# A decoder layer on one core: where the down weights' sums are formed, the order of the first gates, and what a later pool's tiles wait for

## The chip, the core and the metric

The kernel runs on one core of a Trainium2 chip. The metric is the time of one execution on the device, in microseconds: the median of three runs is 1895.49 us (1895.41 to 1898.42). The engines are TensorE (PE in the rows; PEld is its loading of weights), VectorE (DVE), ScalarE (ACT), GpSimd (POOL) and SyncE (SP), which only issues DMAs. Each engine works through its instructions in order; an instruction that waits holds all that stand behind it on that engine, the DMAs that the engine issues included.

## The reference, cut to what matters

One layer of a decoder, 1024 positions by 1024 channels, in float32. The first sub-layer normalises x, runs four causal mixers (A: sparse attention, B: dilated windows, C: forgetting attention, D: latent attention), and then gates, sums and projects their outputs. The second is a gated feed-forward network with a causal convolution of width 3.

```python
h = rms_norm(x, g1)
o = [A(h), B(h), C(h), D(h)]                       # 256, 128, 256, 256 channels
merged = sum(sigmoid(h @ w_gate[i]) * (o[i] @ w_branch[i]) for i in range(4))
x = x + rms_norm(merged @ w_out, g2)
f = rms_norm(x, g3)
up, gate = split(f @ w_up)                         # 2816 channels each
y = activation(causal_conv3(gate)) * up
x = x + rms_norm(y @ w_down, g4)
```

## The kernel before, in words

Every product is kept near float32: each operand is split into a high part (a cast to fp32r on ACT, `split_weights`) and a low part (raw minus high, on DVE or POOL), and three matmuls stand for one (`gemm`). Activations are held with channels on the partitions; a matmul has 128 channels in, 128 out and 512 positions.

**Stage 1, the attention** (pool `attn`), has a prologue in which h is formed, the projections run and the keys and queries are prepared, and then the softmax blocks of the four mixers. Where TensorE would stand, it takes matmuls of the fillers: `fill_tile` computes one tile of branch 1's gates (48 matmuls `pf`), with its weights loaded by SP, cast by ACT (`fh`), and their low part `fl` formed by POOL; the tanh goes to `gate_d` in memory. There are eight; they have low priority, and what is left of them is done at the end of the stage.

**The sums for the last product.** The feed-forward network's down projection is done in a form with fewer products, which needs sums and differences of quarters of its weights. `down_sums` (L218 to L231) forms them ahead on POOL, in the prologue of stage 1: for each of 11 blocks two loads of 128x1024 (`draw`, L224), four operations of 128x512 (L226 to L229) and two stores into `wt_d` (L231). The tiles have the tags `whi` and `wlo` of the pool of weights, two buffers each.

**Stage 2, the gates** (pool `p2`). It begins with branch 1, whose gates are loaded back from `gate_d` (`te`, L1118, into tiles of the tag "c", four buffers); `add_branch` multiplies with the branch's weights and adds into `merged` by one DVE operation (STT, L1008). `load_output` (L984 to L991) brings a mixer's output: a load into `oraw` (one buffer, issued by ACT), a cast `oh` (ACT) and `ol` (DVE). Two tiles of branch 3 have plain gates (`plain`, L1111 and L1122 to L1130). `make_sums` (L1045 to L1072) forms sums of quarters of h on DVE. Then come pairs j = 1 to 11, each two gate tiles by seven products in place of eight: X[j] (gx, two products), gy (S2, S3), gz (S1, A22), gw (S4), then the branch product gp. `gate_sets(j+1)` (L1023 to L1036) is prepared meanwhile: sums of the raw gate weights on POOL (s1 L1028, L1029, L1030, L1035), casts on ACT (L960), low parts on POOL or DVE (L961), in six slots. Pairs 4 and 8 begin a new branch and load its output first.

**Stages 3 and 4** (pools `p3`, `p4`) are the output projection with norm and residual, and the feed-forward network; the last product reads `wt_d`.

What is written in the program is then put in order for each engine by a scheduler with priorities. A tile of a pool that opens later waits until the earlier pool whose memory it takes is done as a whole.

Of the kernel before, what the change touches and what calls it, by code (L numbers as in the profile page):

```python
# [15 lines left out]
F32 = mybir.dt.float32  # L16
# [3 lines left out]
ALU = mybir.AluOpType  # L20
# [3 lines left out]
D = 1024  # L24
# [62 lines left out]
def body(tc, a, out):  # L87
# [31 lines left out]
    def split_weights(hi, lo, raw, eng, scale):  # L119
        if scale == 1.0:  # L120
            A.copy(hi, raw)  # L121
            eng.tensor_tensor(lo, raw, hi.bitcast(F32), op=ALU.subtract)  # L122
        else:
            A.mul(hi, raw, scale)
            eng.tensor_scalar(raw, raw, scale, None, op0=ALU.mult)
            eng.tensor_tensor(lo, raw, hi.bitcast(F32), op=ALU.subtract)

    def load_weights(src, shape, pool_=None, scale=1.0, eng=None):

        pool_ = pool_ or wp  # L130
# [43 lines left out]
    def h_half(hf):  # L174
        return lambda kt: (H[hf][0][:, kt], H[hf][1][:, kt])


    with ExitStack() as c1:
# [36 lines left out]
            if i is not None:  # L215
                fill_tile(i)

        def down_sums(jj):  # L218


            w = [wp.tile([128, D], F32, name="draw", tag=("whi", "wlo")[jj % 2], bufs=2) for _ in range(2)]
            for c in range(2):
                f = 128 * (NH * c + jj)
                G.dma_start(w[c], a["wdn"][f:f + 128, :])  # L224
            l, r = slice(0, 512), slice(512, 1024)
            G.tensor_tensor(w[1][:, r], w[1][:, r], w[0][:, r], op=ALU.subtract)  # L226
            G.tensor_tensor(w[0][:, r], w[0][:, r], w[0][:, l], op=ALU.subtract)
            G.tensor_tensor(w[0][:, l], w[0][:, l], w[1][:, r], op=ALU.add)
            G.tensor_tensor(w[1][:, l], w[0][:, l], w[1][:, l], op=ALU.subtract)  # L229
            for c in range(2):  # L230
                G.dma_start(wt_d[jj][c], w[c])  # L231


        def weights_tm(src):

# [77 lines left out]
            SP.dma_start(t, bass.AP(tensor=src.tensor, offset=src.offset + 127, ap=[[1280, 128], [1, 1152]]))  # L313
            return t

        def project(src, scale=1.0, eng=G):

            hi, lo = load_weights(src, [KT, 128], scale=scale, eng=eng)
            for hf in range(2):
                ps = bank()  # L320
                gemm(ps, lambda kt: (hi[:, kt, :], lo[:, kt, :]), h_half(hf), range(KT))
                yield hf, ps
# [193 lines left out]
        KCL = ap.tile([128, 64], F32R, name="KCL")  # L516
        VC = ap.tile([128, 128], F32R, name="VC")
        kvc = ap.tile([128, S], F32, name="kvc", tag="vt", bufs=BUFS["vt"])
        for hf, ps in project(a["win"][0], eng=V):
            A.copy(kvc[:, cs(hf)], ps)  # L520
        blk = [tile4("blk", "vs", (128, 16, 2, 64), F32) for _ in range(2)]
        posT = ap.tile([128, 32], F32, name="posT")
# [9 lines left out]
        for e in range(2):  # L532
            G.memset(blk[e], 0.0)
            for d in range(2):
                r = slice(64 * d, 64 * d + 64)
                V.tensor_tensor(blk[e][r, :, d, 0:63], kv3[r, :, e:e + 63],
                                posT[r, 16 * e:16 * e + 16].unsqueeze(2).to_broadcast([64, 16, 63]), op=ALU.add)
        for jj in range(NH):
            down_sums(jj)
        fill()  # L540

        for i in range(4):
            V.tensor_copy(sm[:, 2 * i:2 * i + 2], tm[i][:, :, 128:176])
        qn = [(tile4("qnhi", "qs"), tile4("qnlo", "qs")) for _ in range(2)]
        lss = ap.tile([128, 2, 8], F32, name="lss")
        kinds = ((0, 128, [kvn], 2), (176, 256, qn, 0))
# [6 lines left out]
        for i, (c0, n, dst, gc) in enumerate(kinds):  # L553
            for b in range(8):
                t = tm[b // 2][:, b % 2, c0:c0 + n]
                V.tensor_scalar(t, t, lss[:, i, b:b + 1], None, op0=ALU.mult)
        for i, (c0, n, dst, gc) in enumerate(kinds):
            for k in range(n // 128):
                for hb in range(2):
# [8 lines left out]

        rotate(sm[:, :, None, 0:32], (0, 8, 1), ap.tile([128, 4, 128], F32, name="rt", tag="th", bufs=BUFS["th"]))

        krt = wp.tile([128, 8, 96], F32, name="krt", tag="wraw", bufs=2)
        V.memset(krt[:, :, 0:64], 0.0)
        V.tensor_copy(krt[:, :, 64:96], sm[:, :, 0:32])
        krt2 = tile4("kr", "vt")
        kr = [krt2[64:96], krt2[96:128]]
# [6 lines left out]
        wkv = tile4("wkv", "P", (128, 2, 512))  # L582
        raw = wp.tile([128, 512], F32, name="wraw", tag="wraw", bufs=2)
        SP.dma_start(raw, a["wukv"])
        split_weights(wkv[:, 0], wkv[:, 1], raw, V, 1.0)
        wq = [tile4("wq", "P", (128, 2, 384)) for _ in range(2)]
        raw = wp.tile([128, 2, 384], F32, name="wraw", tag="wraw", bufs=2)
        SP.dma_start(raw, a["wuq"])
        split_weights(wq[0], wq[1], raw, V, 1.0)

        gate = ap.tile([128, 8, 12], F32, name="gate")
        A.activation(gate, sm[:, :, 32:44], AF.Tanh, scale=0.5)
# [320 lines left out]
        A.dma_start(o_d[256:384, :], ot0)  # L913


    hq = ctx.enter_context(pool("hq"))
    merged = [hq.tile([128, KT, 512], F32, name=f"mg{hf}", tag="g", bufs=2) for hf in range(2)]
    psq = ctx.enter_context(pool("psq", space=PSUM))

    def pq(name, tag="q"):  # L920
        return psq.tile([128, D], F32, name=name, tag=tag, bufs=2)
# [44 lines left out]
        gemm(ps, lambda k: (t[:, 0, 128 * k:128 * k + 128], t[:, 1, 128 * k:128 * k + 128]),  # L966
             lambda k: (bh[:, k], bl[:, k]), range(4))

    with pool("p2") as p2:
        branches = ((1, 256, 1), (3, 640, 2), (0, 0, 2), (2, 384, 2))  # L970
        kt0 = {br: f0 // 128 for br, f0, _ in branches}
        O, pairs = {}, [(br, p) for br in (3, 0, 2) for p in range(4)]
# [28 lines left out]
        def add_branch(br, m, hf, t, pb, bw, nk):  # L1001


            c = slice(512 * hf, 512 * hf + 512)
            gemm(pb, lambda k: (bw[0][:, m % 2, k], bw[1][:, m % 2, k]),
                 lambda k: (O[br, k][0][:, c], O[br, k][1][:, c]), range(nk))
            if br == 1:
                V.scalar_tensor_tensor(merged[hf][:, m], t, 1.0, pb, op0=ALU.add, op1=ALU.mult)  # L1008
            else:
                V.scalar_tensor_tensor(t, t, 1.0, pb, op0=ALU.add, op1=ALU.mult)  # L1010
                V.tensor_tensor(merged[hf][:, m], merged[hf][:, m], t, op=ALU.add)

        def raw_gates(j):
            if j not in raws and j < len(pairs):
# [93 lines left out]

        lo_f, hi_f = slice(0, 512), slice(512, 1024)
        load_output(*branches[0])  # L1110
        plain = [load_weights(a["wg"][3, m], [KT, 128]) for m in range(2)]  # L1111
        for p in range(4):
            bw = branch_weights(1, p, 1)
            for m in (2 * p, 2 * p + 1):
# [4 lines left out]
                    add_branch(1, m, hf, t, ps[:, (lo_f, hi_f)[hf]], bw, 1)  # L1119
        load_output(*branches[1])  # L1120
        bw = branch_weights(3, 0, 2)
        for m, (gh, gl) in enumerate(plain):  # L1122
            for hf in range(2):
                ps = pq("pgb", "qr"[hf])
                gemm(ps[:, lo_f], lambda k: (gh[:, k], gl[:, k]), h_half(hf), range(KT))
                t = c_tile("tg")
                A.activation(t, ps[:, lo_f], AF.Tanh, scale=0.5)
                add_branch(3, m, hf, t, ps[:, hi_f], bw, 2)
# [18 lines left out]
        for _ in range(2):
            load_wo()

# [3 lines left out]

    hs = ctx.enter_context(pool("hs"))

    def operand(t):
        return t[:, 0:4], t[:, 4:8]

    B = {"11": None, "21": operand(hs.tile([128, KT, 512], F32R, name="b21"))}
    with pool("p3") as p3:

        def put(jobs):

# [149 lines left out]
        put([job("2", 3), job("3", 3)])  # L1315
        put([job("1", 3), job("4", 3)])

    with pool("p4") as p4:
        slot_p4 = lambda: p4.tile([128, 2, 512], F32R, name="aset", tag="as", bufs=8)
        cw = p4.tile([128, 2 * NJ, 4], F32, name="cw")  # L1320
        SP.dma_start(cw, a["convw"])
# [298 lines left out]
```

## Time and profile before

| | |
|---|---|
| median of three runs | 1895.49 us (1895.41 to 1898.42) |
| profiled execution | 1898.08 us, span 1896.3 us |
| granted clock of TensorE, mean | 0.972 |
| PE busy | 1794.0 us (95%) |
| DVE, ACT, POOL busy | 1275.2, 850.5, 648.6 us |
| DMA | 180.09 MB, mean 95 GB/s |

The span is the time from the first to the last instruction; the run is 1.8 us longer. Busy times overlap. PE is the engine with the most work by far, so a microsecond counts where PE stands or runs at a lower granted clock. The granted clock has two levels, 1.2 and 2.4 GHz; 0.74 for a stretch means that about half of it was at the lower one. In the rows, "idle before <- releaser" is time in which an engine had nothing to do until the named instruction was done.

### The profile page before, as it was taken

Reading aid. Unit: us, or ns where it says so; the run is one execution under the profiler, and the core shown is the slowest. Engines: PE = TensorE matmul, PEld = TensorE weight load, DVE = VectorE, ACT = ScalarE, POOL = GpSimd, SP = SyncE. Lnnn points to the kernel's source line nnn. Section 1 sums busy time; section 2 is a strip of 40 time slices with the busy share of each in tenths; the row PEclk is TensorE's granted clock in tenths of the full one; section 3 lists DMA queues with packets and bytes.
Section 4 is the critical chain, followed back from the end, with each engine's and each line's share of the span. In section 5 each row is a group of like instructions: output and inputs, shape, how many; then the busy total and the mean of one; then the engine's idle time right before and its main releaser. Section 6 shows DMA issues by size and latency. Waiting matters only on the chain. (4 is left out here: it accounts for less than half of the span.)

```text
span 1896.3 us, 24478 instructions
## 1 busy us (share of the span) xinstructions
PE 1794.0 (95%) x8644; PEld 1453.3 (77%) x8644; DVE 1275.2 (67%) x2413; ACT 850.5 (45%) x1622; POOL 648.6 (34%) x638
## 2 busy tenths in 40 slices
PE   8885999999999999788999999989999999999997
PEld 7754777777777778566888888778888888888886
DVE  5535886999888626384555565669767676677757
ACT  5323555665666545133333343444434344454444
POOL 1347522121111230106444410248676767400110
PEclk9877999999999999999999999989999999999999
DMA  7178311010001111332211123232222222194235
GB/s 261 60 227 269 141 46 47 25 58 13 24 22 47 61 45 35 108 125 63 74 60 53 59 93 141 78 102 78 80 87 78 90 78 84 57 332 125 88 105 183
DMA packets 70634, 180.09 MB, mean 95 GB/s; under 512 B 11040, under 2 KB 16496, under 8 KB 70512
## 3 DMA queue, kind: packets, MB, share of 16 engines
q1 hardware_dynamic: 50992, 121.73, 19.9%
q10 hardware_dynamic: 13184, 33.73, 4.9%
q0 software_dynamic: 6336, 23.07, 3.5%
q8 instruction: 68, 1.11, 0.2%
q14 instruction: 54, 0.44, 0.1%
HBM read 139.09 MB, written 43.67 MB: 96 GB/s over the span
## 5 line engine op out<-in xcount | busy, mean ns | idle before, releaser
L411 ACT ACTIVATE P<-P,nm 128x512 f32<-128x512 f32 (+7 forms) x160 | 107.9, 676 | 65.6 <-DVE nm L406 64.8
L449 ACT CAST th<-ptp 128x512 fp32r<-128x512 f32 (+3 forms) x202 | 97.1, 518 | 83.8 <-PE ptp L443 72.3
L1251 POOL TENSOR_TENSOR aset<-sums,aset 128x512 fp32r<-128x512 f32 x66 | 129.7, 1965 | 7.3 <-ACT aset L1250 6.8
L144 PE MATMUL pd<-hh,whi 128*128 128x512 f32 x320 | 129.3, 404 | 2.0 <-DVE kl L344 2.0
L450 DVE TENSOR_TENSOR tl<-ptp,th 128x512 fp32r<-128x512 f32 (+3 forms) x202 | 115.5, 600 | 21.0 <-ACT th L449 18.9
L146 PE MATMUL pd<-hh,wlo 128*128 128x512 f32 x320 | 129.2, 404 | 0.0
L145 PE MATMUL pd<-hl,whi 128*128 128x512 f32 x320 | 127.8, 399 | 0.0
L443 PE MATMUL ptp<-miscc,P 128*128 128x128 f32 x678 | 114.1, 277 | 10.7 <-DVE P L420 4.8
L1474 PE MATMUL pk<-aset 128*128 128x512 f32 x308 | 120.3, 394 | 1.2 <-DVE part L1554 0.8
L1475 PE MATMUL pk<-aset 128*128 128x512 f32 x308 | 120.3, 390 | 1.3 <-DVE aset L122 1.1
L1476 PE MATMUL pk<-aset 128*128 128x512 f32 x308 | 119.5, 390 | 0.0
L447 POOL MEMSET th<- 128x128 f32 x86 | 19.2, 224 | 272.9 <-PE pvt L458 121.8
L1250 ACT CAST aset<-wraw 128x512 fp32r<-128x512 f32 x88 | 54.0, 617 | 101.1 <-PE pz L146 37.4
L443 PEld LDWEIGHTS ptp<-miscc,P 128*128 128x128 f32 x678 | 81.1, 142 | 23.5 <-DVE P L420 6.6
L1250 ACT CAST aset<-sums 128x512 fp32r<-128x512 f32 x66 | 40.7, 620 | 120.3 <-PE py L146 32.8
L121 ACT CAST aset<-r 128x512 fp32r<-128x512 f32 x77 | 47.7, 620 | 97.6 <-PE pk L1476 87.6
L122 DVE TENSOR_TENSOR aset<-r,aset 128x512 fp32r<-128x512 f32 x77 | 55.5, 721 | 51.4 <-ACT aset L121 51.4
L960 ACT CAST aset<-wraw 128x512 fp32r<-128x512 f32 x66 | 40.7, 621 | 99.4 <-PE gx L146 41.2
L1266 POOL TENSOR_TENSOR sums<-wraw 128x512 f32<-128x512 f32 x22 | 30.8, 1402 | 127.9 <-PE pk L146 101.4
L961 POOL TENSOR_TENSOR aset<-wraw,aset 128x512 fp32r<-128x512 f32 x33 | 43.7, 1325 | 89.5 <-ACT aset L960 89.5
L458 PE MATMUL pvt<-th,vs 128*128 128x256 f32 x238 | 69.2, 303 | 2.8 <-DVE ot L468 2.5
L1474 PEld LDWEIGHTS pk<-aset 128*128 128x128 f32 x308 | 57.8, 188 | 17.3 <-DVE part L1554 1.5
(451 smaller groups left out, 5679.2 us busy)
## 6 DMA issues: line engine op xcount, KB each, us to landing
wraw<-in_wup SPq DMA_DIRECT2D x44, 512.0 KB, 3.6
wraw<-in_wg SPq DMA_DIRECT2D x24, 512.0 KB, 3.5
draw<-in_wdn POOLq DMA_DIRECT2D x22, 512.0 KB, 4.4
wt_d<-draw POOLq DMA_DIRECT2D x22, 512.0 KB, 3.8
act_d<-o ACTq DMA_DIRECT2D x22, 512.0 KB, 3.7
r<-act_d SPq DMA_DIRECT2D x44, 256.0 KB, 5.4
wraw<-wt_d SPq DMA_DIRECT2D x44, 256.0 KB, 2.6
wraw<-in_win SPq DMA_DIRECT2D x20, 512.0 KB, 3.3
```

The costliest lines, as they stand in the source:

```text
L144: T.matmul(ps, lh, rh, start=first and ii == 0, stop=False)
L145: T.matmul(ps, lh, rl, start=False, stop=False)
L146: T.matmul(ps, ll, rh, start=False, stop=last and ii == n - 1)
L411: A.activation(P[:, 0:c0], P[:, 0:c0], AF.Exp, bias=prev, scale=-1.0, accum_out=den)
L443: T.transpose(tp[0:kr, at[x]], P2[x[1]][:, c:c + kr], ident)
L449: A.copy(th[0:kr, i0:i1], tp[0:kr, i0:i1])
L450: V.tensor_tensor(tl[0:kr, i0:i1], tp[0:kr, i0:i1], th[0:kr, i0:i1].bitcast(F32), op=ALU.subtract)
L1250: A.copy(t[:, 0], src)
L1251: eng.tensor_tensor(t[:, 1], src, t[:, 0].bitcast(F32), op=ALU.subtract)
L1474: T.matmul(ps[b], at[:, 0, c], wt[:, 0], start=st, stop=False, skip_group_check=not first)
L1475: T.matmul(ps[b], at[:, 0, c], wt[:, 1], start=False, stop=False, skip_group_check=not first)
L1476: T.matmul(ps[b], at[:, 1, c], wt[:, 0], start=False, stop=sp, skip_group_check=not first)
```

## The change

Four things are changed; the arithmetic stays the same.

1. `down_sums` leaves the prologue. It is called in stage 2 after each pair, for two halves at a time, 22 in all. A half works in one tile of 128x4x256 of the tag `oraw`, which has one buffer and is also that of `load_output`: two loads, four operations of 128x256, two stores, all issued by POOL. Rows in memory are 1 KB long instead of 4 KB, and there are 88 DMAs of 256 KB instead of 44 of 512 KB.
2. In the prologue some copies, half of the scalings of `tm`, a memset and the low parts of three weights go from DVE to POOL; `krt` takes the tag `whi`.
3. The plain gates of branch 3, m = 0, are computed ahead of branch 1's additions; their results stay in PSUM and in two of the four "c" tiles until branch 3. `make_sums` is called ahead of branch 1, and the weights of m = 1 are loaded after it.
4. The pools `hq`, `psq`, `p2`, `hs`, `p3` and `p4` are opened with `reuse_waits="tile"`: a tile waits only for the tiles whose memory it takes.

```diff
-        def down_sums(jj):
-            w = [wp.tile([128, D], F32, name="draw", tag=("whi", "wlo")[jj % 2], bufs=2) for _ in range(2)]
...
-        for jj in range(NH):
-            down_sums(jj)
         fill()
         for i in range(4):
-            V.tensor_copy(sm[:, 2 * i:2 * i + 2], tm[i][:, :, 128:176])
+            G.tensor_copy(sm[:, 2 * i:2 * i + 2], tm[i][:, :, 128:176])
...
                 t = tm[b // 2][:, b % 2, c0:c0 + n]
-                V.tensor_scalar(t, t, lss[:, i, b:b + 1], None, op0=ALU.mult)
+                (G if b % 2 else V).tensor_scalar(t, t, lss[:, i, b:b + 1], None, op0=ALU.mult)
...
-        krt = wp.tile([128, 8, 96], F32, name="krt", tag="wraw", bufs=2)
-        V.memset(krt[:, :, 0:64], 0.0)
+        krt = wp.tile([128, 8, 96], F32, name="krt", tag="whi", bufs=2)
+        G.memset(krt[:, :, 0:64], 0.0)
...
-        split_weights(wkv[:, 0], wkv[:, 1], raw, V, 1.0)
+        split_weights(wkv[:, 0], wkv[:, 1], raw, G, 1.0)
...
-        split_weights(wq[0], wq[1], raw, V, 1.0)
+        split_weights(wq[0], wq[1], raw, G, 1.0)
...
-    hq = ctx.enter_context(pool("hq"))
+    hq = ctx.enter_context(pool("hq", reuse_waits="tile"))
...
+        sums_of = iter((jj, u) for jj in range(NH) for u in range(2))
+        def down_sums(n):
+            for jj, u in [next(sums_of) for _ in range(n)]:
+                w = p2.tile([128, 4, 256], F32, name="draw", tag="oraw", bufs=1)
+                cols = lambda x: x.rearrange("p (h u t) -> p h u t", h=2, u=2)[:, :, u]
+                for c in range(2):
+                    f = 128 * (NH * c + jj)
+                    G.dma_start(w[:, 2 * c:2 * c + 2], cols(a["wdn"][f:f + 128, :]))
+                G.tensor_tensor(w[:, 3], w[:, 3], w[:, 1], op=ALU.subtract)
+                G.tensor_tensor(w[:, 1], w[:, 1], w[:, 0], op=ALU.subtract)
+                G.tensor_tensor(w[:, 0], w[:, 0], w[:, 3], op=ALU.add)
+                G.tensor_tensor(w[:, 2], w[:, 0], w[:, 2], op=ALU.subtract)
+                for c in range(2):
+                    G.dma_start(cols(wt_d[jj][c]), w[:, 2 * c:2 * c + 2])
...
-        plain = [load_weights(a["wg"][3, m], [KT, 128]) for m in range(2)]
+        def plain_gates(m):
+            gh, gl = load_weights(a["wg"][3, m], [KT, 128])
+            t = []
+            for hf in range(2):
+                ps = pq("pgb", "qr"[hf])
+                gemm(ps[:, lo_f], lambda k: (gh[:, k], gl[:, k]), h_half(hf), range(KT))
+                t.append((ps, c_tile("tg")))
+                A.activation(t[hf][1], ps[:, lo_f], AF.Tanh, scale=0.5)
+            return t
+        first = plain_gates(0)
+        T1, T2, T3, t4 = make_sums()
         for p in range(4):
             bw = branch_weights(1, p, 1)
...
-        for m, (gh, gl) in enumerate(plain):
...
-            if m == 0:
-                T1, T2, T3, t4 = make_sums()
+        for hf, (ps, t) in enumerate(first):
+            add_branch(3, 0, hf, t, ps[:, hi_f], bw, 2)
+        gh, gl = load_weights(a["wg"][3, 1], [KT, 128])
...
             combine(j)
+            down_sums(2)
```

The other pools of point 4 change in the same way, and `project` loses its argument `eng` (the first projection's weights are split on POOL, too).

How this moves instructions on POOL in the gate stage: before, one pair's worth of rows between two s1 (`aset` are low parts of the sets, `wraw` the raw gates):

```order
L1028 TENSOR_TENSOR s1_9270<-wraw_9105 128x512
L1029 TENSOR_TENSOR wraw_9105<-wraw_9103,wraw_9105 128x512
L961 TENSOR_TENSOR aset_9100<-wraw_8928,aset_9100 128x512
L1030 TENSOR_TENSOR wraw_9103<-s1_9270,wraw_9103 128x512
L1035 TENSOR_TENSOR wraw_9103<-wraw_9103 128x512
L961 TENSOR_TENSOR aset_9274<-wraw_9103,aset_9274 128x512
L961 TENSOR_TENSOR aset_9277<-wraw_9105,aset_9277 128x512
L961 TENSOR_TENSOR aset_9280<-s1_9270,aset_9280 128x512
```

Now, while the set of pair 6 is prepared (`draw` is a half, `wt_d` its store):

```order
L1031 TENSOR_TENSOR wraw_9234<-s1_9407,wraw_9234 128x512
L1012 DMA wt_d4_95<-draw_9551 256x1x256
L1036 TENSOR_TENSOR wraw_9234<-wraw_9234 128x512
L1006 DMA draw_9560<-in_wdn 128x2x256 x2
L944 TENSOR_TENSOR aset_9411<-wraw_9234,aset_9411 128x512
L1007 TENSOR_TENSOR draw_9560<-draw_9560 128x256
L944 TENSOR_TENSOR aset_9414<-wraw_9236,aset_9414 128x512
L1008 TENSOR_TENSOR draw_9560<-draw_9560 128x256
L1009 TENSOR_TENSOR draw_9560<-draw_9560 128x256
L1010 TENSOR_TENSOR draw_9560<-draw_9560 128x256
L1012 DMA wt_d4_95<-draw_9560 256x1x256 x2
L944 TENSOR_TENSOR aset_9417<-s1_9407,aset_9417 128x512
```

Of the operations of a set, some now stand between a half's loads and its stores, and s1 of the next set stands behind whole halves.

And on DVE at the start of stage 2: before, STTs of branch 1 (`mg`) and operations of `make_sums` (`t`) take turns from the beginning:

```order
L1047 TENSOR_TENSOR t_8562<-hh1_128,hl1_129 128x2048
L1047 TENSOR_TENSOR t_8563<-hh0_126,hl0_127 128x2048
L122 TENSOR_TENSOR ol_8326<-oraw_8323,oh_8325 128x1024
L122 TENSOR_TENSOR bw_8343<-bw_8341,bw_8342 128x256
L1048 TENSOR_TENSOR t_8563<-t_8562,t_8563 128x2048
L1008 SCALAR_TENSOR_TENSOR mg0_8315<-te_8349,pgb_8348 128x512
L1008 SCALAR_TENSOR_TENSOR mg0_8315<-te_8362,pgb_8361 128x512
L1047 TENSOR_TENSOR t_8564<-hh1_128,hl1_129 128x2048
L1008 SCALAR_TENSOR_TENSOR mg1_8316<-te_8355,pgb_8348 128x512
L1008 SCALAR_TENSOR_TENSOR mg1_8316<-te_8368,pgb_8361 128x512
```

Now the operations of `make_sums` come in a block:

```order
L1049 TENSOR_TENSOR t_8287<-t_8281,t_8279 128x1024
L1048 TENSOR_TENSOR t_8288<-hh0_126,hl0_127 128x1024
L1049 TENSOR_TENSOR t_8281<-t_8281,t_8280 128x2048
L1049 TENSOR_TENSOR t_8294<-t_8280,t_8293 128x2048
L1049 TENSOR_TENSOR t_8288<-t_8288,t_8281 128x1024
L1048 TENSOR_TENSOR t_8289<-hh0_126,hl0_127 128x1024
L1049 TENSOR_TENSOR t_8302<-t_8281,t_8301 128x2048
L1049 TENSOR_TENSOR t_8289<-t_8289,t_8281 128x1024
L122 TENSOR_TENSOR bw_8313<-bw_8311,bw_8312 128x256
L1049 TENSOR_TENSOR t_8306<-t_8286,t_8305 128x1024
L1049 TENSOR_TENSOR t_8306<-t_8287,t_8305 128x1024
L991 SCALAR_TENSOR_TENSOR mg0_8205<-te_8319,pgb_8318 128x512
```

They stand ahead of the first STT, behind `ol`.

## Rows read from the trace of the kernel before

**Rows 1.** Stretches: length, busy us (instructions) of five engines, clock, DMA share, GB per second

```profile
40.00:60.00 20.00, 19.97 (x108) 17.96 (x107) 6.51 (x11) 6.07 (x15) 1.29 (x1) 1.00 0.23 76
100.00:200.00 100.00, 69.42 (x263) 50.88 (x262) 49.31 (x107) 27.93 (x63) 64.24 (x71) 0.74 0.75 245
...
900.00:1200.00 300.00, 300.00 (x1320) 244.23 (x1320) 165.40 (x239) 111.14 (x186) 91.09 (x67) 1.00 0.25 81
1200.00:1300.00 100.00, 91.92 (x419) 75.31 (x418) 75.75 (x87) 43.39 (x78) 53.10 (x39) 0.93 0.24 80
```

**Rows 2.** TensorE's waits, 0 to 215 us: line, waited for, us in total, times, longest

```profile
PE pf L146 <- POOL fl L122: 6.4, 1, 6.4
PE pd L144 <- DVE vd L679: 6.1, 2, 5.0
PE pd L635 <- DVE u L630: 5.7, 1, 5.7
```

**Rows 3.** Timeline of POOL in the prologue: start, us, engine, line, operation, [idle before]

```profile
75.53 1.48 POOL L224 DMA_DIRECT2D draw<-in_wdn  x2 [9.45 <-PE pd L146]
79.92 1.78 POOL L226 TENSOR_TENSOR draw<-draw 128x512 f32<-128x512 f32 x1 [2.91 <-DMA draw<-in_wdn]
...
89.66 1.10 POOL L231 DMA_DIRECT2D wt_d<-draw  x2
...
92.92 0.57 POOL L224 DMA_DIRECT2D draw<-in_wdn  x1 [0.86 <-DMA wt_d<-draw]
...
160.16 1.31 POOL L228 TENSOR_TENSOR draw<-draw 128x512 f32<-128x512 f32 x1
```

**Rows 4.** Timeline of DVE in the prologue

```profile
156.53 0.28 DVE L508 TENSOR_TENSOR rt<-qt,rot 128x128 f32<-128x128 f32 x1
...
159.79 1.84 DVE L508 TENSOR_TENSOR rt<-qt,rot 128x128 f32<-128x128 f32 x1
```

**Rows 5.** POOL's groups by line and shape: busy us, mean ns, idle before

```profile
L122 POOL TENSOR_TENSOR wlo<-wraw,whi 128x1024 fp32r<-128x1024 f32 x12 | 28.8, 2398 | 53.6 <-ACT whi L121 48.2 <-ACT P L411 5.4
```

**Rows 6.** Timelines of PE and DVE in branch 1, and the group of its STT

```profile
801.85 1.22 PE L144 MATMUL pgb<-oh,bw 128*128 128x512 f32 x2 [8.14 <-ACT oh L121]
...
803.31 2.28 DVE L1048 TENSOR_TENSOR t<-t 128x2048 f32<-128x2048 f32 x1
...
829.26 1.23 DVE L122 TENSOR_TENSOR ol<-oraw,oh 128x1024 fp32r<-128x1024 f32 x1
...
L1008 DVE SCALAR_TENSOR_TENSOR mg<-te,pgb x16: 679/680/689, 805.5 to 827.9; 128x512 f32<-128x512 f32 x16
```

**Rows 7.** DMA issues by form (page), and the answer for tile te: us to landing

```profile
wraw<-in_wg SPq DMA_DIRECT2D x24, 512.0 KB, 3.5
...
wraw<-wt_d SPq DMA_DIRECT2D x44, 256.0 KB, 2.6
...
DMA to landing us min/median/max: 2.5/2.8/4.6
```

**Rows 8.** Timelines of PE and POOL at the first pair

```profile
851.21 0.39 PE L144 MATMUL gx<-hh,aset 128*128 128x512 f32 x1
...
863.98 1.26 POOL L961 TENSOR_TENSOR aset<-wraw,aset 128x512 fp32r<-128x512 f32 x1
```

**Rows 9.** Timelines of POOL and PE in the steady gate stage

```profile
979.53 1.30 POOL L1028 TENSOR_TENSOR s<-wraw 128x512 f32<-128x512 f32 x1
980.91 1.82 POOL L1029 TENSOR_TENSOR wraw<-wraw 128x512 f32<-128x512 f32 x1
...
1004.28 1.29 POOL L1028 TENSOR_TENSOR s<-wraw 128x512 f32<-128x512 f32 x1
...
1001.94 0.39 PE L144 MATMUL gw<-hh,aset 128*128 128x512 f32 x1
...
1010.37 0.39 PE L144 MATMUL gx<-hh,aset 128*128 128x512 f32 x1
```

**Rows 10.** TensorE's waits, 1200 to 1290 us

```profile
PE tp L1169 <- DVE t L1173: 4.2, 2, 2.1
```

More of the change, by code (lines that the diff above doesn't have):

```diff
@@ L216, in fill @@
                 fill_tile(i)
-        def down_sums(jj):
-            w = [wp.tile([128, D], F32, name="draw", tag=("whi", "wlo")[jj % 2], bufs=2) for _ in range(2)]
[L222 to L231, printed above, removed]
         def weights_tm(src):
@@ L314, in toeplitz, with project @@
             return t
-        def project(src, scale=1.0, eng=G):
-            hi, lo = load_weights(src, [KT, 128], scale=scale, eng=eng)
+        def project(src, scale=1.0):
+            hi, lo = load_weights(src, [KT, 128], scale=scale, eng=G)
             for hf in range(2):
@@ L518, in body @@
         kvc = ap.tile([128, S], F32, name="kvc", tag="vt", bufs=BUFS["vt"])
-        for hf, ps in project(a["win"][0], eng=V):
+        for hf, ps in project(a["win"][0]):
             A.copy(kvc[:, cs(hf)], ps)
@@ L913, in body @@
         A.dma_start(o_d[256:384, :], ot0)
-    hq = ctx.enter_context(pool("hq"))
+    hq = ctx.enter_context(pool("hq", reuse_waits="tile"))
     merged = [hq.tile([128, KT, 512], F32, name=f"mg{hf}", tag="g", bufs=2) for hf in range(2)]
-    psq = ctx.enter_context(pool("psq", space=PSUM))
+    psq = ctx.enter_context(pool("psq", space=PSUM, reuse_waits="tile"))
     def pq(name, tag="q"):
@@ L967, in product @@
              lambda k: (bh[:, k], bl[:, k]), range(4))
-    with pool("p2") as p2:
+    with pool("p2", reuse_waits="tile") as p2:
         branches = ((1, 256, 1), (3, 640, 2), (0, 0, 2), (2, 384, 2))
@@ L1121, in body @@
         bw = branch_weights(3, 0, 2)
-        for m, (gh, gl) in enumerate(plain):
[L1123 to L1128, printed above, removed]
-            if m == 0:
-                T1, T2, T3, t4 = make_sums()
+        for hf, (ps, t) in enumerate(first):
+            add_branch(3, 0, hf, t, ps[:, hi_f], bw, 2)
+        gh, gl = load_weights(a["wg"][3, 1], [KT, 128])
+        for hf in range(2):
+            ps = pq("pgb", "qr"[hf])
+            gemm(ps[:, lo_f], lambda k: (gh[:, k], gl[:, k]), h_half(hf), range(KT))
+            t = c_tile("tg")
+            A.activation(t, ps[:, lo_f], AF.Tanh, scale=0.5)
+            add_branch(3, 1, hf, t, ps[:, hi_f], bw, 2)
         raw_gates(1)
@@ L1150, in body @@
         m0 = merged_block(0, wp)
-    hs = ctx.enter_context(pool("hs"))
+    hs = ctx.enter_context(pool("hs", reuse_waits="tile"))
     def operand(t):
@@ L1161, in body @@
     B = {"11": None, "21": operand(hs.tile([128, KT, 512], F32R, name="b21"))}
-    with pool("p3") as p3:
+    with pool("p3", reuse_waits="tile") as p3:
         def put(jobs):
@@ L1316, in body @@
         put([job("1", 3), job("4", 3)])
-    with pool("p4") as p4:
+    with pool("p4", reuse_waits="tile") as p4:
         slot_p4 = lambda: p4.tile([128, 2, 512], F32R, name="aset", tag="as", bufs=8)
```

## The prediction

> **What bounds the kernel now.** I read the table of stages first, then TensorE's waits in the first 215 us, the timelines of GpSimd and VectorE there, and last the timelines around the start and in the middle of the gate stage. The page has TensorE (PE) busy for 1794.0 of 1896.3 us, so the rest is some 102 us plus what a half clock costs. From 900 to 1200 us, the steady gate stage, PE is busy for 300.00 of 300.00 us [rows 1]: work added to another engine costs nothing there until PE has to wait for it. In 100 to 200 us PE issued 263 matmuls; at the rate of 40 to 60 us (108 in 20 us) or of the gate stage (1320 in 300 us) these are 49 to 60 us of work, so 40 to 51 us are lost in that stretch, and the granted clock was 0.74 [rows 1]. The fillers (gate tiles of branch 1 that PE runs in the holes of the attention stage) end at 801.85 - 8.14 = 793.7 us [rows 6]; I call that moment F. PE's work before F is the same in both kernels, so a hole closed in the prologue brings F forward by its length.
>
> **What goes: the sums in the prologue.** The 22 loads, 44 subtractions and additions and 22 stores keep GpSimd (POOL) busy for 44 x 1.3 + 44 x 0.55 = 81 us, and move 23 MB. What this costs PE: it waits 6.4 us for `fl`, which stands on POOL behind the sums [rows 2, 3]; and 6.1 us for `vd`, work of VectorE (DVE) [rows 2]. DVE rows are stretched while POOL computes: the same L508 took 0.28 us at 156.53 and 1.84 us at 159.79, with L228 on POOL from 160.16 [rows 3, 4]. The DMA share is 0.75 there, against 0.23 in 40 to 60 us [rows 1]. Other waits are chains of data that stay, as that for `u`, 5.7 us [rows 2]. Of the 40 to 51 us I take 32 back: 45 less 10 for such chains and 3 for the work that POOL gets in exchange (eight scalings, copies, three splits, of which a 128x1024 costs 2.4 us [rows 5]). Bounds: 15 (the waits for `fl` and `vd` and a few stretched rows) and 45. **Term A: -32 (-45 to -15).**
>
> The Trainium skill ("SBUF — State Buffer", Who interferes with whom) states that a VectorE instruction with two SBUF inputs and a GpSimd instruction that reads SBUF exclude each other for a whole instruction. The stretched L508 agrees (1.84 against 0.28). It speaks against the change as well as for it, since the same operations now run beside VectorE's gate work; what that would cost is worked out from rows in rival 1 (C of 35 in place of 16).
>
> **What moves to the start of the gate stage.** Before, PE stood 8.14 us for the first `oh` [rows 6]. After, plain gates of branch 3, m = 0 (48 matmuls at 0.23 us, 11 us), stand in that hole; they are only brought forward. But they hold two of the four "c" tiles until branch 3's own addition, so the loads `te` of branch 1 have two tiles. SP queues each `te` behind the STT (L1008) that frees a tile: two at a time, 2.8 us landing [rows 7] + 0.68 us [rows 6] = 3.5 us for two of 16. Besides, thirteen operations of the sums, four like the row of 2.28 us and eight of half its size [rows 6] and one small, 18 us in all, now stand on DVE between `ol` (near F + 8.6; before, `oh` was there at F + 8.1) and the first STT: F + 26.8. The 16 STTs end near 26.8 + 0.7 + 7.5 x 3.5 = F + 53.7; before at 828.6, F + 34.9 [rows 6]. Then come `ol` 1.2 [rows 6], the second `oraw` load 3.5 [rows 7], a cast and `ol`, 2.4: F + 60.8; and branch 3, m = 1. First gx: near F + 66, before 851.2 = F + 57.5 [rows 8]. The raw gates land near F + 69.8, as their buffer is free only after the last plain gemm. POOL has meanwhile started the first half of the sums (it may, once `oraw` is free at F + 60.8) and stands before s1 in a wait for that half's store until F + 69.5; then one load issue and seven operations of 1.3 to 1.8 us up to the third low part: F + 80.8, against 865.2 = F + 71.5 before [rows 8]. **Term B: +9 (+5 to +14).** PE idles over 5 us twice on the way; I add 3 us for matmuls at half clock after such holes (100 to 200 us shows what holes do to the clock [rows 1]), 0 to 6.
>
> **What moves into the gate stage.** One half is, in order and without overlap, since there is one buffer: two loads, four operations, two stores, and the next half's loads wait on POOL for the stores. From rows: two 512 KB loads took 75.53 to 79.92 = 4.4 us, two stores 89.66 to 92.92 = 3.3 us [rows 3]; a 256 KB transfer of SP lands 0.9 us sooner than a 512 KB one (2.6 against 3.5 [rows 7]), so 3.5 and 2.4. A 128x256 operation isn't in the trace: 1.31 us at 512 and 2.40 at 1024 columns [rows 3, 5] give an estimate of 0.76. One half: 3.5 + 4 x 0.75 + 2.4 = 8.9 us. With 4.4 and 3.3 it is 10.7; with 0.9 off each side once more, as if the size alone counted, 7.1.
>
> The period of a pair is 24.74 us (979.53 to 1004.28), in which POOL has eight operations, 11 us [rows 9]. With gx at T, S4 is multiplied at T + 16.3 (1001.94, gx 24.74 before 1010.37) [rows 9]. The order puts 8 halves between the branch's `ol` (T + 9 of pair 4 and again of pair 8) and the low part of S4 of the fourth pair, and 25 operations of the sets among them, some 14 of which lie in no wait: 8 x 8.9 + 14 x 1.3 + 9 = 98.4, and PE wants it at 3 x 24.74 + 16.3 = 90.5. So PE waits 7.9 us in each block, 8h - 63.3 for a half of h us; nothing below 7.9, 21 us at 10.5. For pairs 1 to 3 (six halves, from F + 60.8) the same count comes out about level. ACT's `oraw` load for branch 2 stands in order behind the eighth store too and holds the casts behind it, 1 us more at most here. **Term C: +16 (0 to +45).**
>
> The Trainium skill ("DMA: Bandwidth & Descriptors", Anatomy of one DMA — SWDGE) gives 2.0 us + bytes / 436 GB/s for one transfer issued by GpSimd: 2.6 us for 256 KB, and 3.2 for 512 KB, where the rows give 3.7 for the second load and 2.7 for the second store. By it a half would take 0.55 + 2.6 + 3.0 + 0.55 + 2.6 = 9.3 us, and term C would be +22 instead of +16.
>
> **Pools that wait tile by tile.** In 1200 to 1300 us 8.1 us are idle; half of them are one wait of TensorE, 4.2 us for `t` on DVE [rows 1, 10], data of the residual and its norm. Weights may come earlier, the chain stays. **Term D: -4 (-8 to 0).** The added DMAs (88 for 44, same bytes) meet a DMA share of 0.25 [rows 1]: nothing.
>
> **Sum.** -32 + 9 + 3 + 16 - 4 = -8 us on the profiled execution's 1898.1 (span 1896.3 and 1.8 around it): 1890. The median of the runs is 1895.5, 2.6 us lower; from it, 1887.5. I say 1887.
>
> **Rivals.**
> 1. *POOL becomes the bound of the gate stage* (slower). The mechanism is h alone: from h = 9.4 (C = +24) the change is level, at 10.5 C is 41 and the time 1912. For it: a price that rests on a subtraction; a first operation that took 1.78 us at 79.92 [rows 3], and L1029 takes 1.82 us beside DVE's work where L1028 takes 1.30 [rows 9]; were all four operations held so, h would be 10.1 and C 2 x 17.5 = 35. Against: DMA share 0.25 there. Chance 0.23.
> 2. *The prologue is bound by its own chains of data.* Then A is -15, and the sum -15 + 28 - 4 = +9: 1904, or 1889 if the halves hide besides. For it: different waits, none above 6.4 us [rows 2]. Against: POOL 64 and DMA 75 of 100 us busy in just that stretch [rows 1]. Chance 0.18.
> 3. *The halves hide and the prologue comes back whole*: h below 8, A -40: -40 + 9 + 3 - 4 = -32, 1863. For it: the order has much of POOL's set work inside the halves' waits. Chance 0.21.
> My forecast, 1872 to 1891.7, has 0.38.
>
> **Numbers.** Runs of this kernel lie within 3 us; 0.2% (3.8 us) is about what can be told from no change: same is 1891.7 to 1899.3. Faster: forecast 0.38, rival 3 0.21, and 0.02 of rival 2: 0.61. Slower: 0.21 of rival 1 and 0.04 of rival 2: 0.25; same, with the rest of these two: 0.14. The range reaches to rival 3 with half a spread and to rival 1 at h = 10.5: 1854 to 1912; the likeliest case alone is 1872 to 1891.7.
>
> **What will show it.** A: F near 762, and 100 to 200 us with a granted clock over 0.85, L508 at 0.28 throughout; wrong if PE still issues under 310 matmuls there. B: STTs of branch 1 in twos every 3.4 us, and 75 to 81 us from F to gy (72 before). C: POOL busy or waiting in DMA throughout the gate stage; PE's waits for POOL's low parts of S4 near the ends of pairs 7 and 11, some 8 us each; h read from the distance of two first loads. If h is above 9.5, the forecast fails by C; if F moves by less than 20, by A. D: the wait for `t` remains.

## The result, and the profile after

The changed kernel takes 1952.94 us (median of 4 runs, 1951.85 to 1954.46) against 1895.79 for the kernel before in the same series: a ratio of 1.0299, 95% interval 1.0281 to 1.0317. It is 57 us slower, where 8 us faster was forecast and the range ended at 1912. The profiled execution's span grew by 56.4 us, from 1896.3 to 1952.7.

Four moments of TensorE divide the span: the last filler, the gx of the first and of the second pair, and the first matmul of the output projection (pk). For the changed kernel, in the timeline of PE (start, length, engine, line, tile; the first row is the last matmul of the last filler, which ends at F):

```profile
752.68 0.40 PE L146 MATMUL pf<-hh,fl 128*128 128x512 f32 x1
...
824.01 0.39 PE L144 MATMUL gx<-hh,aset 128*128 128x512 f32 x1
...
864.10 0.39 PE L144 MATMUL gx<-hh,aset 128*128 128x512 f32 x1
...
1194.58 0.39 PE L144 MATMUL pk<-woh,mh 128*128 128x512 f32 x1
```

For the kernel before, in the same view, the two that [rows 8] does not have:

```profile
886.66 0.40 PE L144 MATMUL gx<-hh,aset 128*128 128x512 f32 x1
...
1134.06 0.39 PE L144 MATMUL pk<-woh,mh 128*128 128x512 f32 x1
```

| stretch | before | after | difference | forecast |
|---|---|---|---|---|
| start to the last filler (F) | 793.7 | 753.1 | -40.6 | -32 |
| F to the gx of pair 2 | 93.0 | 111.0 | +18.1 | +9 + 3 |
| gx of pair 2 to the first pk | 247.4 | 330.5 | +83.1 | +16 |
| first pk to the end | 762.2 | 758.1 | -4.1 | -4 |

The prologue gave more than was forecast, and the gate stage lost five times what was. The table of stretches of the changed kernel (length, busy us of PE, PEld, DVE, ACT, POOL, then clock, DMA share, GB/s) answers to [rows 1]; the third line is the same stage in the kernel before:

```profile
100.00:200.00 100.00, 92.50 (x462) 71.78 (x461) 64.21 (x179) 48.37 (x102) 14.07 (x21) 0.93 0.31 85
864.10:1194.58 330.48, 272.07 (x1081) 215.89 (x1080) 165.52 (x198) 82.73 (x138) 214.94 (x229) 0.91 0.36 114
886.66:1134.06 247.40, 247.40 (x1082) 201.25 (x1081) 133.68 (x198) 87.44 (x137) 96.26 (x71) 1.00 0.22 67
```

In 100 to 200 us PE now issues 462 matmuls instead of 263, at a clock of 0.93 instead of 0.74. In the gate stage it is busy for 272.1 of 330.5 us, where it had no gap before. So 58 of the 83 us lost are waits; the other 25 are the same matmuls taking longer, at a granted clock of 0.91 instead of 1.00. POOL is at 215 of 330 us, its issues included, without the time in which it stands in its queue. TensorE's waits there (line, waited for, us in total, times, longest):

```profile
PE gp L144 <- DVE v L993: 23.5, 7, 5.9
PE gw L146 <- POOL aset L944: 19.4, 6, 7.0
PE gw L144 <- DVE u L1090: 15.4, 3, 7.7
```

The low parts `aset` come late from POOL. The waits for `v` and `u`, two thirds of the sum, go by way of ACT. In pair 6 (timelines of ACT, DVE and PE), DVE had `v` ready at 1002.5 us, but its tanh ran only at 1016.09: ACT stood for POOL's `wraw`, and two casts of the next set came first. DVE's low part waited for such a cast and took 3.42 us, `v`'s STT stood behind it, and the product gp waited for that STT:

```profile
1013.99 1.14 ACT L943 CAST aset<-wraw 128x512 fp32r<-128x512 f32 x2 [20.47 <-POOL wraw L1031]
...
1017.30 3.42 DVE L944 TENSOR_TENSOR aset<-wraw,aset 128x512 fp32r<-128x512 f32 x1 [4.55 <-ACT aset L943]
...
1021.97 0.79 PE L144 MATMUL gp<-oh,bw 128*128 128x512 f32 x1 [5.92 <-DVE v L993]
```

Pairs 2, 5, 9 and 10 show the same chain. The two longest waits for `u` stand behind ACT's casts, too: in pair 7 ACT had stood 16.6 us for a half's store, in pair 11 14.3 us for the load of the output projection's weights.

What a half costs is in POOL's timeline, at a place with no other work inside:

```profile
954.08 1.47 POOL L1006 DMA_DIRECT2D draw<-in_wdn  x2
958.46 0.73 POOL L1007 TENSOR_TENSOR draw<-draw 128x256 f32<-128x256 f32 x1 [2.90 <-DMA draw<-in_wdn]
...
960.89 1.07 POOL L1010 TENSOR_TENSOR draw<-draw 128x256 f32<-128x256 f32 x1
961.91 1.43 POOL L1012 DMA_DIRECT2D wt_d<-draw  x2
966.03 1.45 POOL L1006 DMA_DIRECT2D draw<-in_wdn  x2 [2.69 <-DMA wt_d<-draw]
```

Two loads are issued in 1.47 us, and the first operation, which needs both, starts at 958.46, 4.38 us after the first issue. The four operations take 3.45 us, with 0.81 us from start to start and 1.07 us for the last; from the first store to the next load, which needs both stores, it is 4.12 us. One half is 954.08 to 966.03 = 11.95 us, against 8.9 in the forecast. The next half with nothing inside, from 994.21 us, takes 11.35. The page has the landings of a single transfer:

```profile
draw<-in_wdn POOLq DMA_DIRECT2D x44, 256.0 KB, 3.2
wt_d<-draw POOLq DMA_DIRECT2D x44, 256.0 KB, 2.6
```

At the start of the stage, DVE's timeline and the group of the STT (duration ns, first and last start) answer to [rows 6]:

```profile
760.15 1.23 DVE L122 TENSOR_TENSOR ol<-oraw,oh 128x1024 fp32r<-128x1024 f32 x1 [25.33 <-ACT oh L121]
...
L991 DVE SCALAR_TENSOR_TENSOR mg<-te,pgb x16: 679/688/690, 780.4 to 810.3; 128x512 f32<-128x512 f32 x16
```

The first STT starts at F + 27.3 (forecast 26.8) and the last ends at F + 57.9 (53.7). In the prologue the operation that was L508 in [rows 4] is L493 now, and none of its four is stretched (min/median/max in ns):

```profile
L493 DVE TENSOR_TENSOR rt<-qt,rot x4: 274/282/286, 142.2 to 149.8; 128x128 f32<-128x128 f32 x4
```

and of TensorE's waits up to 215 us [rows 2] the one for `fl` is gone, and those for `vd` and `u` are down from 6.1 and 5.7 us:

```profile
PE pd L144 <- DVE vd L662: 3.0, 3, 1.3
...
PE pd L618 <- DVE u L613: 1.6, 1, 1.6
```

### The profile page after: what moved, and what is told of

It reads as the page before. It is cut to its first block, busy times and chain, and to the rows that moved or that the text cites. A ratio compares the mean times of both kernels' runs of the same rounds, so it can differ in the third digit from the quotient of the medians.

```text
span 1952.7 us, 24561 instructions
## 1 busy us (share of the span) xinstructions
PE 1804.5 (92%) x8644; PEld 1458.1 (75%) x8644; DVE 1289.3 (66%) x2397; ACT 846.3 (43%) x1622; POOL 715.9 (37%) x742
## 5 line engine op out<-in xcount | busy, mean ns | idle before, releaser
L1265 POOL TENSOR_TENSOR aset<-sums,aset 128x512 fp32r<-128x512 f32 x66 | 125.1, 1896 | 8.1 <-ACT aset L1264 8.0
L943 ACT CAST aset<-wraw 128x512 fp32r<-128x512 f32 x66 | 39.6, 617 | 163.8 <-POOL wraw L1031 79.5
L944 DVE TENSOR_TENSOR aset<-wraw,aset 128x512 fp32r<-128x512 f32 x33 | 39.2, 1191 | 82.7 <-ACT aset L943 77.0
L122 POOL TENSOR_TENSOR fl<-fraw,fh 128x512 fp32r<-128x512 f32 x16 | 23.2, 1450 | 132.9 <-ACT fh L121 99.8
L444 PE MATMUL pvt<-tl,vs 128*64 128x256 f32 x286 | 69.4, 289 | 2.2 <-POOL tl L433 1.8
```

The source lines that it names most:

```text
L1265: eng.tensor_tensor(t[:, 1], src, t[:, 0].bitcast(F32), op=ALU.subtract)
```

## The experiments

Each row is one profiled execution, divided as above; times in us. The last column is the median of 4 runs for the kernel before, the changed kernel and the last two rows, and a single run for the others; the profiled execution of the last row took 1879.1 us. Beside the single runs the kernel before took 1899.2 us (sums back, only moved, SP, rows of 2 KB) and 1900.0 us (oraw, plain gates, prologue's work, and a run below) on the same chip; beside the last three 1898.0 (median of 7). The kernel before thus differs by 4 us between series (1895.8 to 1900.0), and smaller differences between rows of different series tell nothing.

| run | F | F to gx 1 | F to gx 2 | gx 2 to pk | pk to end | time |
|---|---|---|---|---|---|---|
| before | 793.7 | 57.5 | 93.0 | 247.4 | 762.2 | 1895.8 |
| changed | 753.1 | 70.9 | 111.0 | 330.5 | 758.1 | 1952.9 |
| sums back in the prologue | 794.6 | 73.8 | 108.8 | 247.2 | 761.9 | 1914.3 |
| only the sums moved | 745.3 | 56.3 | 100.8 | 327.6 | 758.1 | 1933.6 |
| transfers issued by SP | 750.6 | 71.1 | 110.7 | 269.0 | 760.8 | 1892.8 |
| rows of 2 KB | 757.7 | 70.3 | 109.3 | 317.4 | 759.8 | 1945.9 |
| oraw loaded by POOL | 754.3 | 70.3 | 110.2 | 327.7 | 760.0 | 1954.0 |
| plain gates back | 757.1 | 54.4 | 98.8 | 330.3 | 759.9 | 1947.8 |
| prologue's work back on DVE | 744.7 | 70.2 | 110.4 | 327.5 | 760.0 | 1944.3 |
| five blocks in the prologue, twelve halves | 769.8 | 56.6 | 101.4 | 257.8 | 761.3 | 1892.1 |
| only the sums moved, SP | 747.7 | 56.8 | 98.3 | 279.2 | 758.5 | 1885.2 |
| the same with tile-wise pools | 743.6 | 55.3 | 94.6 | 278.1 | 761.0 | 1883.7 |

**Sums back in the prologue.**

```diff
+        for jj in range(NH):
+            down_sums(jj)
...
-            down_sums(2)
```

> The changed kernel with the sums formed in the prologue again, whole blocks as before; the plain gates ahead, the work moved to GpSimd and the tile-wise pools stay. Theory 1 (the halves on GpSimd are the whole loss; one takes 12 us): the eleven pairs go back to 24.7 us each (gate stage 247 us from the gx of pair 2 to the first pk, 331 in the changed kernel), the fillers' end goes back to about 790 us (753 in the changed kernel), and what the plain gates ahead cost stays: 1895 + 10 to 18 - 4 = 1900 to 1910 us. Theory 2 (the new order of the first gates and ACT's held loads make the gate stage slow): the gate stage stays above 300 us and the time above 1940.

1914.3 us. The gate stage is back at 24.7 us for every pair, PE busy without a gap, and the prologue as slow as before:

```profile
100.00:200.00 100.00, 65.14 (x225) 48.44 (x224) 26.18 (x47) 18.38 (x41) 69.16 (x76) 0.76 0.78 259
900.00:1100.00 200.00, 200.00 (x875) 162.53 (x874) 106.13 (x159) 67.47 (x108) 87.74 (x65) 1.00 0.21 63
```

All of the gate stage's loss is the halves'; what the new order of the first gates costs stays, 16 us up to the second gx. The time is 4 us over the expected band of theory 1, with the kernel before 3 us slower in this series too.

**Only the sums moved**, in the kernel before.

> The kernel before with one part of the change: the sums by halves in the gate stage. Theory 1: fillers end near 757 us, first gx 57 us after them as before, the gate stage takes 320 to 335 us: 1895 - 37 + 80 = 1925 to 1945 us. Theory 2: the gate stage is within 260 us, 1865 to 1880.

1933.6 us, in the expected band, though the last filler ends 12 us earlier than was expected. The prologue is better than in the changed kernel, the pairs as slow:

```profile
100.00:200.00 100.00, 94.18 (x505) 75.25 (x503) 66.86 (x180) 51.07 (x107) 14.20 (x24) 0.97 0.30 83
900.00:1100.00 200.00, 170.91 (x705) 136.54 (x704) 104.83 (x132) 53.07 (x89) 135.37 (x143) 0.94 0.34 110
```

**Transfers issued by SP.**

```diff
-                    G.dma_start(w[:, 2 * c:2 * c + 2], cols(a["wdn"][f:f + 128, :]))
+                    SP.dma_start(w[:, 2 * c:2 * c + 2], cols(a["wdn"][f:f + 128, :]))
...
-                    G.dma_start(cols(wt_d[jj][c]), w[:, 2 * c:2 * c + 2])
+                    SP.dma_start(cols(wt_d[jj][c]), w[:, 2 * c:2 * c + 2])
```

> The changed kernel with the loads and stores of the halves issued by SyncE instead of GpSimd; the four operations stay on GpSimd. Theory 1 (GpSimd stands in the queue behind its own loads and stores): GpSimd has only 3 us for a half, the gate stage falls from 331 to 250 to 275 us, 1875 to 1895 us in all. Rival (the chain of one buffer, load, four operations, store, is the bound wherever it is issued, and now holds SyncE's loads of raw gates): the gate stage stays above 300 us, over 1925.

1892.8 us: some 60 us come back from the issuing engine alone. The chain of the one buffer is shorter by 2 us; SP's timeline (the stores of a half, then the next one's loads) shows 10.0 us from one half's loads to the next one's:

```profile
949.88 1.38 SPq L1012 DMA_DIRECT2D wt_d<-draw  x2
953.24 1.25 SPq L1006 DMA_DIRECT2D draw<-in_wdn  x2
959.90 1.38 SPq L1012 DMA_DIRECT2D wt_d<-draw  x2
963.24 1.25 SPq L1006 DMA_DIRECT2D draw<-in_wdn  x2
```

What changed besides is who stands in it: SP waits for the stores, POOL only for the loads. POOL's waits for halves from 850 to 1150 us, here and then in the changed kernel:

```profile
POOL draw L1007 <- DMA draw<-in_wdn: 55.6, 20, 5.8
...
POOL draw L1007 <- DMA draw<-in_wdn: 37.8, 18, 3.9
POOL draw L1006 <- DMA wt_d<-draw: 19.1, 9, 2.8
```

POOL is also rid of 88 issues of 0.74 us, some 65 us. The run doesn't separate this from the shorter chain: by the prediction's 8h - 63.3, 2 us less for a half would be 16 us in each of the two blocks.

**Rows of 2 KB.**

```diff
-                cols = lambda x: x.rearrange("p (h u t) -> p h u t", h=2, u=2)[:, :, u]
+                cols = lambda x: x[:, 512 * u:512 * u + 512]
...
```

Bytes, transfers and operations stay as many; the operations combine other columns than the sums need.

> The changed kernel with halves taken as 512 neighbouring columns: rows of 2 KB and 128 of them in a transfer, in place of 1 KB and 256; same bytes, same count of transfers and operations (the operations then combine other columns than they should). Theory 1a (short rows make the issue 0.74 instead of 0.57 us and the landings 4.4 and 4.1 instead of 3.5 and 2.4): a half takes 9 to 10 us and the gate stage falls to 270 to 295 us, 1890 to 1915. Theory 1b (the landings are long for another reason, as the waits in two directions of one queue): a half stays near 12 us, over 1940.

1945.9 us: theory 1b. The issue is shorter, the landing is not:

```profile
953.63 1.10 POOL L1006 DMA_DIRECT2D draw<-in_wdn  x2
957.64 0.73 POOL L1007 TENSOR_TENSOR draw<-draw 128x256 f32<-128x256 f32 x1 [2.90 <-DMA draw<-in_wdn]
...
965.14 1.11 POOL L1006 DMA_DIRECT2D draw<-in_wdn  x2 [2.73 <-DMA wt_d<-draw]
```

Two issues take 1.10 instead of 1.47 us; then the loads need the same 2.90 us and the stores 2.73 instead of 2.69. The half here is 11.5 us, and the gate stage 13 us shorter.

**oraw loaded by POOL.**

```diff
-                load_output(*[b for b in branches if b[0] == br][0])
+                load_output(*[b for b in branches if b[0] == br][0], eng=G)
```

> The changed kernel with the loads of oraw for pairs 4 and 8 issued by GpSimd instead of ScalarE, so that ScalarE is not held by the wait for the halves' stores (21.5 and 16.6 us in the profile of the changed kernel). Theory 1 (the chain of halves on GpSimd delays the sets; ScalarE's wait only lies beside it): the gate stage stays at 315 to 335 us. Theory 2 (ScalarE's held queue is a loss of its own): it falls by 20 to 38 us, to 293 to 311.

The gate stage stays at 327.7 us: theory 1. ACT's two waits for stores are gone and it waits for POOL's `wraw`, the sums for the sets, instead (its waits, 800 to 1200 us; 79.5 us in the changed kernel):

```profile
ACT aset L943 <- POOL wraw L1031: 93.9, 7, 19.7
```

**Plain gates back**, with `make_sums`, where they were before.

> The changed kernel with the plain gates and make_sums where they were before; halves on GpSimd stay. Theory (two c tiles and the block of sums on VectorE delay the first pair): the first gx comes 56 to 58 us after the last filler instead of 70.9, the second 98 to 103 after instead of 111, and the time falls by 8 to 13 us to 1940 to 1945. Rival (the start is bound by the first half of the sums on GpSimd): the second gx stays 108 us or more after the last filler, 1950 or more.

The first gx starts 54.4 us after the last filler, the second 98.8 after; 12 us of the start were the two "c" tiles and the block on DVE. The time falls by only 5 us, short of the expected 8 to 13. The last filler ends 4 us later, within the spread of the five kernels with this prologue (750.6 to 757.7 us):

```profile
811.49 0.39 PE L144 MATMUL gx<-hh,aset 128*128 128x512 f32 x1
```

**Prologue's work back on DVE.**

> The changed kernel with the work that moved from VectorE to GpSimd in the prologue moved back (copies, scalings, memset, three splits, krt's tag). Theory (this move costs: the last filler ended at 745.3 us in the kernel with the sums' move alone, at 753.1 in the changed one): last filler near 745, time 1944 to 1948. Rival (the difference is the tile-wise pools or the new gates): the last filler stays at 751 to 754.

The last filler ends at 744.7 us and the time falls by 8.6 us, as expected. The four kernels without the sums and with this work on DVE end it at 743.6 to 747.7 us, the five with it on POOL at 750.6 to 757.7: handing copies, scalings and splits to POOL cost some 8 us, and in the kernel with the sums in the prologue it had brought nothing (794.6 against 793.7).

```profile
744.25 0.40 PE L146 MATMUL pf<-hh,fl 128*128 128x512 f32 x1
```

**Sums late in the attention stage.** The kernel before, whole blocks, called after the last projection of mixer B, SP issuing.

```diff
...
         vb = v_pair(a["win"][13])
+        for jj in range(NH):
+            down_sums(jj)
...
```

> The kernel before with the sums in whole blocks as there, but after the last projection of the attention stage (in mixer B), with SyncE issuing their loads and stores. Theory 1 (the prologue is free of them, and GpSimd has room in mixer B, where it is under a quarter busy): last filler 745 to 760 us, gate stage 247 us, 1848 to 1865 us in all. Rival (GpSimd stands in the sums' waits while TensorE needs its memsets and low parts in mixer B): last filler at 775 or later, 1878 or more.

1910.7 us: far over what was expected and in the rival's band, but not by the rival's cause. The fillers are used up at 664 us here, so the run has no row in the table. The prologue is as good as in the other kernels without the sums (clock 0.98 from 100 to 200 us), but in mixer B a hole of 33 us opens (table of stretches), in which PE waits once for `whi`, the weights of a projection:

```profile
650.00:700.00 50.00, 17.38 (x54) 12.35 (x55) 0.00 (x0) 3.30 (x4) 32.47 (x23) 0.66 0.59 215
```

PE's waits, 500 to 900 us:

```profile
PE pd L144 <- ACT whi L121: 27.7, 1, 27.7
```

The reason is the buffers: `draw` has the tags `whi` and `wlo`, and the cast that makes these weights waits for the stores of the sums (ACT's timeline):

```profile
691.00 1.04 ACT L121 CAST whi<-wraw 128x1024 fp32r<-128x1024 f32 x1 [25.96 <-DMA wt_d<-draw]
```

**Five blocks in the prologue, twelve halves.** The kernel before; one half for each pair and one more in pair 3, POOL issuing.

> The kernel before with five of the eleven blocks of sums in the prologue as before and the other six as twelve halves in the gate stage, one for each pair and one more in pair 3, GpSimd issuing. Theory 1 (a block of four pairs loses 8 x 12 less the room of 63 us; with 4 halves the sum 4 x 12 + 27 = 75 is under 90.5): the gate stage goes back to 247 to 252 us although GpSimd still issues and waits; last filler at 765 to 772 us, as five elevenths of the gain of 48 are given back: 1868 to 1882 us. Rival (each half on GpSimd holds TensorE, whatever the room): the gate stage keeps half of the 80 us, 285 or more, and the time is over 1900.

The halves are as long as in the changed kernel (12.0 and 12.4 us from loads to loads), yet the gate stage is 257.8 us:

```profile
946.41 1.46 POOL L1023 DMA_DIRECT2D draw<-in_wdn  x2
...
958.40 1.44 POOL L1023 DMA_DIRECT2D draw<-in_wdn  x2 [2.70 <-DMA wt_d<-draw]
...
970.83 1.47 POOL L1023 DMA_DIRECT2D draw<-in_wdn  x2 [1.17 <-DMA wt_d<-draw]
```

PE's waits in the pairs (870 to 1130 us) are down to one kind:

```profile
PE gp L144 <- DVE v L1010: 7.8, 4, 3.2
```

It is 6 us over the expected band's end in the gate stage and 10 us over it in all, but nearer to no loss than to the rival's 285. Theory 1 holds in kind, but leaves out these waits for `v`. One run of 1892.1 beside a median of 1898.0 is no clear gain.

**Only the sums moved, SP issuing**, and **the same with tile-wise pools**: four runs each.

> The kernel before with the sums by halves in the gate stage as its one change, SyncE issuing the loads and stores; four operations a half stay on GpSimd. By the terms measured so far: last filler at 745 us, second gx 95 to 101 us after, gate stage 265 to 272 us, 758 to 762 us from the first pk: 1865 to 1880 us, 0.984 to 0.992 of before. Rival (SyncE's queue, not the plain gates, delays the start, so that the 71 us to the first gx stay): 1885 to 1895.

> As the run before it, with the pools that wait tile by tile besides (the changed kernel with SyncE issuing the halves' transfers and with the plain gates, make_sums and the prologue's work on VectorE as before). If tile-wise waits bring a gain of their own, it is 2 to 8 us below the run before it, shown between the first pk and the end or at the first gx; if not, as the tail of 761.9 us with them and the sums in the prologue suggests (762.2 before), within 3 us of it.

The first is at 1885.2 us, a ratio of 0.9935 to the kernel before (0.9914 to 0.9957), the second at 1883.7, 0.9932 (0.9912 to 0.9953). Both beat both kernels, by 13 and 14 us for the one and by some 68 for the other; the first missed its band by 5 us, the gate stage being 279 instead of 272 at most. Its time is in the rival's band, but the rival's cause did not occur: the first gx came 56.8 us after the last filler, not 71. The two are not told apart, so tile-wise waits show no gain of their own. The gate stage of the first:

```profile
846.00:1125.00 279.00, 255.75 (x1080) 206.23 (x1079) 151.29 (x199) 84.39 (x137) 160.27 (x145) 0.96 0.42 131
```

## Why the prediction was wrong

**The price of a half, in term C, failed.** The prediction put it at 8.9 us; it was 11.95 (11.35 in the cheaper half). It was read from rows in which one transfer is waited for, and a half waits for two. The operation at 79.92 [rows 3] did not wait for both loads of 75.53: the second was issued at 76.48 and landed 4.6 us later, at about 81 us. The two stores of 89.66 landed 3.0 and 3.8 us after their issues, and the load at 92.92, with a tile of its own, waited for the first alone (POOL's timeline before, the landing of that load, the landings of the two stores):

```profile
76.48 0.53 POOL L224 DMA_DIRECT2D draw<-in_wdn  x1
DMA to landing us min/median/max: 4.6/4.6/4.6
...
DMA to landing us min/median/max: 3.0/3.4/3.8
```

So two loads of 512 KB took 5.5 us and not 4.4, and the prediction's 3.7 and 2.7 us for the second load and the second store are 4.6 and 3.8. The 0.9 us taken off each side for the smaller size was no error by itself (the profiles' pages have 4.4 us for a load of 512 KB and 3.2 for one of 256 KB, 3.8 and 2.6 for the stores), but it was taken off the price of one transfer. Two loads took 4.38 us against 3.5, two stores up to the next load 4.12 against 2.4, and the four operations 3.45 against 3.0, of which 0.33 is the last one's 1.07 in place of 0.74. Together 0.9 + 1.7 + 0.45 = 3.05 us, which is all of 11.95 - 8.9. The prediction gave h = 9.4 as the point from which the change loses and ended its range at 10.5 us; rival 1 was right in kind, too small in size, and had 0.23.

**The total of term C agrees better than its parts, which is luck in part.** With h = 11.95 the formula 8h - 63.3 gives 32.3 us in each of two blocks; pairs 4 to 7 and 8 to 11 took 33.6 and 34.7 us more than 24.74 each. For pairs 1 to 3 "about level" at 8.9 becomes six halves by 3.05 = 18 us; 14.7 were measured in pairs 2 and 3. But the formula is for the low part of S4 in the fourth pair:

```profile
928.30 0.39 PE L144 MATMUL gx<-hh,aset 128*128 128x512 f32 x1
...
1044.17 0.50 PE L146 MATMUL gw<-hh,aset 128*128 128x512 f32 x1 [2.04 <-POOL aset L944]
...
1060.88 0.39 PE L144 MATMUL gx<-hh,aset 128*128 128x512 f32 x1
```

That matmul went on 115.9 us after the gx of pair 4, 25 us later than the 90.5 at which PE wants it, where the formula gives 122.8, 32 us later. The other 8 us of the block come behind it, from a wait for `u` (4.0 us) and from matmuls at the lower clock. Waits by way of ACT are in term C with 1 us at most, and a price for the lower clock is not in it.

**Term A was right in sign and too small.** The sums' move alone brings 48 us (last filler at 745.3), and 49 with the rest of the change but the prologue's work (744.7); 45 was the upper end of the range. The wait for `u`, counted as a chain that stays, fell from 5.7 to 1.6 us. The change's own second point gave some 8 back; it was counted as 3.

**Term B was half of what came.** The STTs began as forecast and ended 4 us later, gx 1 was 5 us later than F + 66, and the second pair starts 18 us later after F than before, against 9 + 3. Of this the new order of the first gates makes 12 (plain gates back) to 16 (no halves in the stage), the halves the rest.

**Term D has its number by luck.** The tail is 4 us shorter, but it is so without tile-wise pools too (758.1) and is not with them when the sums are in the prologue (761.9) or when SP issues (760.8, 761.0). The prediction took the 4 us from waits, and the wait for `t` stayed at 4.2 us. From the first pk to the end, PE stands for 18.4 us before and 18.6 after; the same matmuls took less time (first before, then after):

```profile
1134.06:1896.30 762.24, 743.84 (x3269) 607.31 (x3267) 540.44 (x693) 332.12 (x548) 306.44 (x230) 0.99 0.33 111
1194.58:1952.70 758.12, 739.54 (x3269) 604.11 (x3267) 544.15 (x692) 331.57 (x547) 306.33 (x230) 0.99 0.33 112
```

In the second 100 us of the tail the granted clock was 0.98 after and 0.94 before; why is open.

The lengthening of POOL's operations by VectorE, the other half of rival 1, is no cause: a half's four operations have medians of 0.73 to 0.74 us (up to 1.6 at times) over the 22 halves, and the estimate was 0.76. VectorE pays instead: the same 198 instructions of the gate stage take 165.5 us in place of 133.7 (134.0 with the sums in the prologue). One of them, the 3.42 us at 1017.30, lies in a chain that TensorE waited for; how much of the loss this makes in all was not separated. Loading oraw from POOL, which frees ACT from the wait for the stores, made the gate stage only 3 us shorter; ACT then waits longer for POOL.

## What to carry to other kernels

A chain through one buffer costs its engine the sum of its latencies when the same engine issues, computes and waits for the store. Count the room of that engine between two due times against it, and read the latency from a row in which the same number of transfers is waited for: look up when each one landed. Moving only the issue to a queue with room gave back 61 of the 83 us of the gate stage. A place with room on the engines is none if the tiles take buffers that the next weights need (sums late in the attention stage). An engine with 60% idle time in the profile has that room only if its work, and that of the engines that wait for it, may be late by that much.

## What the runs showed of the hardware

Of two transfers that POOL issued one behind the other, the second landed 5.5 us after the first issue for 2 x 512 KB (before, from 75.53 to about 81 us), and within 4.4 us for 2 x 256 KB (954.08 to 958.46). The medians of single landings are 4.4 and 3.2 us for loads, 3.8 and 2.6 for stores; the larger ones ran in a stretch with a DMA share of 0.75, the smaller at 0.36. An issue took 0.74 us (median) for 256 rows of 1 KB, and 0.55 to 0.58 for 128 rows of 2 KB or 4 KB. From the fit in the Trainium skill ("DMA: Bandwidth & Descriptors", Anatomy of one DMA — SWDGE) 2.6 us are estimated for 256 KB and 3.2 for 512 KB. The 2.6 us of the stores of 256 KB agree; the other three medians are longer.
